# Gelus and casts moved behind the kept sums in three short pairs, and the down projection's sums taken half by half

## The chip, the cores and the metric

The kernel runs on one core of a Trainium2 chip. The metric is the device time of one execution in microseconds (us), as the median of several runs. Five engines work side by side, each through its own list of instructions: TensorE (PE in the profile; PEld is its loading of weights), VectorE (DVE), ScalarE (ACT), GpSimd (POOL) and SyncE (SP), which issues most of the DMAs. Matmuls write into PSUM, eight banks of 512 float32 columns for each of 128 partitions; VectorE and ScalarE read the banks.

## What is computed

One layer of a decoder on 1024 prompt positions and 64 sample positions (T = 1088 columns): attention in a sliding window, a gated branch beside it, and a feed-forward block with a convolution. Only the last one is touched here. From the reference, cut down:

```
def conv_ffn(h, w_up, conv_w, conv_b, w_down, prev):
    z = h @ w_up
    zp = jnp.concatenate([prev, z], axis=1)
    c = conv_b + sum(zp[:, j:j + T] * conv_w[j] for j in range(CONV_W))
    a, b = jnp.split(c, 2, axis=-1)
    return (jax.nn.gelu(a) * b) @ w_down, zp[:, T:]
```

with a model width of 1024, a hidden width of 2 x 2816 and a convolution of width 3. All data are float32.

## The kernel before

**Precision.** Each matmul operand is split into a high and a low part (`split`, line 39): ScalarE casts the high part (line 40), VectorE takes the difference (line 41). Each product is then three matmuls: high by high, high by low, low by high.

**The up projection.** The 2816 hidden rows of each half are 22 tiles of 128 rows; tile f of the first half and tile f of the second make a *pair*, `za` and `zb`. The two are worked out together by a scheme of seven products in place of eight (Winograd's form of Strassen's), in the class `Chain`. A chain works on one group of columns: group 0 has 576 columns (moving operands of 288), group 1 has 512 (moving operands of 256). Product j is 4 x 3 = 12 matmuls (line 301) into one of three PSUM banks, by the letters "adadaca": the first, third, fifth and seventh product add up in bank a, the second and fourth in bank d. Since the third adds to what the first left in a, the first's value has to be copied out before; this is a *kept sum*, copied by ScalarE in `keep` (lines 282 and 284). So the third product waits for the keep of the first, the fourth for that of the second, the fifth for that of the third, and the last for that of the fifth. The other products end in sums of VectorE or GpSimd (line 289) or scaled copies of ScalarE (line 319).

**Pairs with only the second group.** For the pairs f = 0, 1 and 2 (`FEW` is 3) the first group is worked out early, while the second group's input is still being made, and is stored to DRAM (`zd`). In the main loop (line 1756) the pairs go in the order 3 to 8, 0, 9 to 14, 1, 15 to 21, 2. A pair of the main loop runs two chains, 24 matmuls per product; pairs 0, 1 and 2 load their first half back (line 1764) and run the chain of group 1 alone, 12 matmuls per product.

**After each pair** `finish` (line 1729) runs the convolution on `za` and on `zb` (`conv`, line 1678: small copies of state by GpSimd, a scaled copy by ScalarE on line 1683, two steps of VectorE on lines 1684 and 1685), the Gelu of the first (lines 1734 and 1737, ScalarE), the product with the second (lines 1739 and 1740, VectorE), and stores the gated values to DRAM (`td`), at every second pair with the sums that the down projection's scheme of seven needs. `side_loads` issues copies of cache rows from DRAM to DRAM for f = 2 to 9. For the last two pairs `finish` is put off into the down projection.

**The down projection** is again seven passes in place of eight (order 5, 0, 2, 4, 6, 1, 3), each over 11 units. For a unit a tile of gated values is loaded (`t_upto`, line 1588: loads run ahead, then the split into `th` and `tl`) and multiplied with four blocks m of weights, each in two column halves e of 288 and 256 columns (`mm_dn`, line 1803). The first two and the last two units of a pass are taken together, in two rounds `mp` of two blocks each. At the end of a pass `take` (line 1808) adds the banks into the result `x` (VectorE, line 1814); the next pass writes the same banks. `dn_pools` (line 1582) opens the pools for this stage before the last pair of the up projection, loads the first four tiles and splits the first two.

**What sets the order.** The code is traced in order; a framework lays out each engine's list from it, with the code's order as priority and by its own reckoning of when things become ready, and it puts in every wait. `W.get` prepares the weights of coming products, with casts on ScalarE and sums on VectorE, so these stand between the instructions described here. `tc.issue_after(x)` binds what is traced under it to come behind x on x's engine.

Of the kernel before, what the change touches and what calls it, by code (L numbers as in the profile page):

```python
# [6 lines left out]
F32 = mybir.dt.float32  # L7
F32R = mybir.dt.float32r
I32 = mybir.dt.int32
AF = mybir.ActivationFunctionType  # L10
ALU = mybir.AluOpType
# [4 lines left out]
P = 128  # L16
D = 1024
KD = 8
NS = 64
NPR = 1024  # L20
T = NS + NPR
HT = T // 2
# [4 lines left out]
NFF = 22  # L27
# [7 lines left out]
def layer(tc, a):  # L35
    nc = tc.nc
    V, S, G, PE = nc.vector, nc.scalar, nc.gpsimd, nc.tensor

    def split(hi, lo, src):
        S.copy(hi, src)  # L40
        V.tensor_sub(lo, src, hi.bitcast(F32))  # L41
# [5 lines left out]
    with ExitStack() as top:  # L47
# [3 lines left out]
        td = [dram.tile([P, 7, HT], F32, name=f"td_{i}") for i in range(NFF // 2)]  # L51
# [3 lines left out]
        def gap(pool, nbytes):  # L55
            if nbytes:
                pool.tile([P, nbytes // 4], F32, name="gap", bufs=1)
# [195 lines left out]
        def right(stack, name, bufs=1):  # L253
            return stack.enter_context(tc.tile_pool(name=name, bufs=bufs, side="right", reuse_waits="tile"))
# [16 lines left out]
        class Chain:  # L271
# [7 lines left out]
            def keep(self, name, src, by=1.0):  # L279
                t = self.keeps.tile([P, 288], F32, name="k" + name.replace("n", "u"), bufs=3 if name in "un" else 2)[:, :self.n2]  # L280
                if by == 1.0:
                    S.copy(t, src)  # L282
                else:
                    S.activation(t, src, AF.Copy, scale=by)  # L284
                self.kept[name] = t
# [66 lines left out]
        apart = ("g", KD - 1, KD - 1)  # L352
# [6 lines left out]
        with ExitStack() as ph1:  # L359
# [61 lines left out]
            order = [*range(FEW, 9), 0, *range(9, 15), 1, *range(15, NFF), 2]  # L421
# [630 lines left out]
            for at, (pair, gs, whole) in enumerate(seq):  # L1052
                if at == 6:
# [3 lines left out]
                chains = [Chain(g, txa, psa, kpa, lambda e, half, g=g, n2=groups[g]["n"] // 2: (  # L1057
                    (zs[g][e][:, n2 * half:n2 * half + n2], 0, n2),)) for g in gs]
# [390 lines left out]
            held = {}  # L1449
# [11 lines left out]
            for c in range(KD):  # L1461
                for at, go in enumerate(merge(1, c, operand(1)) if c > 1 else [none, none, *first[c][2:]]):
                    if at == 1:
                        t, u = held.pop(c)
# [117 lines left out]
        def dn_pools():  # L1582
            dnp["t"] = right(tops, "tq")
            dnp["s3"] = own["s3"] = right(tops, "s3")
            t_upto(4, 2)
            gap(dnp["t"], 128)

        def t_upto(loads, splits):

            for n in range(len(ts["raw"]), min(loads, 7 * (NFF // 2))):  # L1590
                j, i = DN_ORDER[n // (NFF // 2)], n % (NFF // 2)
                raw = dnp["t"].tile([P, 576], F32, name="traw", bufs=4)[:, :HT]
                nc.sync.dma_start(raw, td[i][:, T_AT[j]])
                ts["raw"].append(raw)
            for n in range(len(ts["made"]), min(splits, 7 * (NFF // 2))):
                th, tl = (dnp["t"].tile([P, 576], F32R, name=x, bufs=5)[:, :HT] for x in ("th", "tl"))
                split(th, tl, ts["raw"][n])
                ts["made"].append((th, tl))
# [3 lines left out]
        def pool2(name, bufs, **kw):  # L1602
            return ph2.enter_context(tc.tile_pool(name=name, bufs=bufs, reuse_waits="tile", **kw))
# [56 lines left out]
        def side_loads(f):  # L1660
            with tc.issue_after(W.last.ins):
                if 2 <= f < 10:
                    nc.sync.dma_start(a["ks"][f - 2], a["ck"][f - 2, 8:128, :])
                    nc.sync.dma_start(a["vso"][f - 2], a["cvd"][f - 2, 8:128, :])
# [10 lines left out]
        def up_chain(g, za, zb):  # L1675
            return Chain(g, tx, psu, up, lambda e, half: z_parts((za, zb)[e], g, half))
# [14 lines left out]
        def z_pair():  # L1691
            return [zp["z"].tile([P, zp["n"]], F32, name=x, bufs=n) for x, n in (("za", zp.get("za", 1)), ("zb", 1))]

        def put_state(f, zs):
            for e, z in enumerate(zs):
                G.tensor_copy(z[:, 0:90].rearrange("p (b t) -> p b t", t=10)[:, :, 0:2],
                              stc[:, f + e * NFF])

        rest = []
        for f in range(FEW):  # L1700
            za, zb = z_pair()
# [18 lines left out]
        tmp = pool2("tmp", 1)  # L1720
# [5 lines left out]

        later, held = [], {}

        def finish(f, za, zb):
            at = order.index(f)  # L1730
            i = at // 2
            ca = conv(f, za)
            gt = za[:, 0:T]
            S.activation(gt[:, NS:T], ca[:, 80:1104], AF.Gelu_apprx_tanh)
            samp = lambda x: x[:, 0:80].rearrange("p (b t) -> p b t", t=10)[:, :, 0:8]
            gts = gt[:, 0:NS].rearrange("p (b t) -> p b t", t=8)
            S.activation(gts, samp(ca), AF.Gelu_apprx_tanh)
            cb = conv(f + NFF, zb)
            V.tensor_mul(gts, samp(cb), gts)
            V.tensor_mul(gt[:, NS:T], cb[:, 80:1104], gt[:, NS:T])  # L1740
            g2 = gt.rearrange("p (h t) -> p h t", h=2)
            if at % 2 == 0:
                nc.sync.dma_start(td[i][:, 0:2], g2)
                held["q"] = g2
            else:
                q, t2 = held["q"], tmp.tile([P, 2, HT], F32, name="t2")
                V.tensor_sub(t2[:, 0], g2[:, 0], g2[:, 1])
                V.tensor_sub(g2[:, 1], q[:, 1], g2[:, 1])
                V.scalar_tensor_tensor(t2[:, 1], g2[:, 1], -1.0, g2[:, 0], ALU.mult, ALU.subtract)
                V.scalar_tensor_tensor(q[:, 0], t2[:, 1], -1.0, q[:, 0], ALU.mult, ALU.subtract)  # L1750
                nc.sync.dma_start(td[i][:, 2:4], g2)
                nc.sync.dma_start(td[i][:, 4:6], t2)
                nc.sync.dma_start(td[i][:, 6], q[:, 0])
            side_loads(f)

        for at, f in enumerate(order):
            if at == NFF - 1:
                t0o.close()
                dn_pools()
                zp.update(z=right(tops, "z2"), za=1)  # L1760
            za, zb = z_pair()
            if f < FEW:
                for e, z in enumerate((za, zb)):
                    nc.sync.dma_start(z[:, 0:594], zd[f][e])
            else:
                put_state(f, (za, zb))
            chains = [up_chain(g, za, zb) for g in ((1,) if f < FEW else (0, 1))]
            for j in range(7):
                w = W.get(3, 1)
                for ch in chains[::1 - 2 * ((7 * at + j) % 2)]:  # L1770
                    ch.product(j, w)
                if f < FEW and j == 3:
                    put_state(f, (za, zb))
            if at < NFF - 2:
                finish(f, za, zb)
            else:
                later.append(lambda f=f, za=za, zb=zb: finish(f, za, zb))
        pse.close()

        with ExitStack() as ph3:  # L1780
# [3 lines left out]
            NU = NFF // 2  # L1784
# [136 lines left out]
            for at, j in enumerate(DN_ORDER):  # L1921
                new, last, n0 = j in (5, 0, 1), at == 6, at * NU
                blocks = [(0, 2), *((x, x + 1) for x in range(2, NU - 4 if last else NU - 2))]
                if not last:
                    blocks.append((NU - 2, NU))
                for lo, hi in blocks:
                    if at == 0:
                        if lo in (2, 5):
                            later.pop(0)()
                        if lo == 8:  # L1930
                            nc.sync.dma_start(a["tails"], stc)
                            ph2.close()
                            own["s2"], own["a22"] = pool3("s2", 1), pool3("a22", 1)
                            xp, lp = pool3("xp", 1), pool3("lp", 1)
                            acc += [lp.tile([P, HT], F32, name=f"acc{th}") for th in range(2)]
                            x_load(0, 0)
                    for go in hooks.get((at, lo), ()):
                        go()
                    got = units(n0 + lo, hi - lo)
                    for mp in range(2) if hi - lo == 2 else (0,):  # L1940
                        for e in range(2):
                            for x in range(lo, hi):
                                for m in range(2 * mp, 2 * mp + 2) if hi - lo == 2 else range(4):
                                    mm_dn(m, e, x, got[x - lo], new)
                        if hi == NU:
                            for m in (2 * mp, 2 * mp + 1):
                                for e in range(2):
                                    take(j, m, e)
            got = units(7 * NU - 4, 4)

# [45 lines left out]
NSTG, FEW, NPRE = 4, 3, 2  # L1996
# [86 lines left out]
```

## Time and profile before

| what | us |
|---|---|
| median of 3 runs | 1504.83 |
| the three runs | 1504.61, 1504.83, 1505.7 |
| the profiled execution, its own time | 1506.5 |
| its span from first to last instruction | 1504.6 |
| TensorE busy in it | 1492.3 |
| VectorE, ScalarE, GpSimd busy | 1163.4, 832.7, 282.5 |

A row of the timeline has the start, the duration, the engine, the line in the kernel, the operation, then output <- inputs with their shapes, and a count where equal instructions follow one another. In square brackets stands how long the engine was idle before, and what it waited for. Pair 0 of the main loop begins at 961 us, pair 1 at 1096, pair 2 at 1251; the down projection starts at 1261. A row of the table by stretches has, for each engine, the busy time and in brackets the number of instructions, then the granted clock, the DMA share and GB/s.

### The profile page before, as it was taken

The numbers are of one execution on the slowest core, as the hardware profiler recorded it, in microseconds if no ns is written. First come the engines' busy times: TensorE is split into PE (matmuls) and PEld (weight loads), VectorE is DVE, ScalarE is ACT, GpSimd is POOL, SyncE is SP. The second block draws the span as 40 slices with busy tenths as digits, with TensorE's granted clock in tenths as the row PEclk, the third lists the DMA queues.
The fourth block names the chain that finished last, engine by engine and source line by source line (L and its number), as shares of the span: only waits on it lengthen the run. The fifth ranks groups of instructions, "written<-read, shape, count | busy, mean of one in ns | idle before, by whom it ended". The sixth has DMA issues, their size and how long they took to land.

```text
span 1504.6 us, 31437 instructions
## 1 busy us (share of the span) xinstructions
PE 1492.3 (99%) x12169; PEld 1479.7 (98%) x12169; DVE 1163.4 (77%) x1954; ACT 832.7 (55%) x1798; POOL 282.5 (19%) x438
## 2 busy tenths in 40 slices
PE   9999999999999999999999999999999999999998
PEld 8999999999998999999999999999999999999998
DVE  6887779557545986988678888898898888785676
ACT  7656674554554775864444654654555556453463
POOL 2001003100030332430222222232142122000003
PEclk9999999999999999999999999999999999999999
DMA  8552468557659757859977423332332217973454
GB/s 282 182 189 104 165 216 270 176 177 249 216 209 326 236 177 237 246 190 315 337 242 271 142 102 121 119 123 95 116 131 95 109 64 243 362 235 98 121 185 134
DMA packets 136932, 286.10 MB, mean 190 GB/s; under 512 B 15312, under 2 KB 43856, under 8 KB 136784
## 3 DMA queue, kind: packets, MB, share of 16 engines
q1 hardware_dynamic: 131952, 279.57, 55.1%
q10 hardware_dynamic: 4832, 4.54, 0.9%
q8 instruction: 95, 1.56, 0.4%
q14 instruction: 53, 0.43, 0.1%
HBM read 195.56 MB, written 90.46 MB: 190 GB/s over the span
## 4 chain that ended last, share of the span: by engine, by line
PE 94%; DVE 3%; ACT 1%; issue 1%; DMA 0%; SPq 0%; DVEq 0%; ACTq 0%
PE st L301 52%; PE mm L241 15%; PE dn L1804 15%; PE st L538 6%; PE sc L1295 1%; PE po L1356 1%; PE mx L904 1%; PE pt L1328 1%; ACT s L1318 1%; DVE nm L1311 0%; DVE s L1321 0%; DVE s L1305 0%; DMA wh<-xt 0%; PE st L603 0%; DVE of L1367 0%
## 5 line engine op out<-in xcount | busy, mean ns | idle before, releaser
L301 PE MATMUL st<-th,wh 128*128 128x256 f32 (+1 forms) x2128 | 611.4, 287 | 0.3 <-ACT k L282 0.2
L301 PE MATMUL st<-tl,wh 128*128 128x256 f32 (+1 forms) x2128 | 609.7, 287 | 0.0
L301 PE MATMUL st<-th,wl 128*128 128x256 f32 (+1 forms) x2128 | 609.3, 286 | 0.0
L301 PEld LDWEIGHTS st<-th,wh 128*128 128x128 f32 x2128 | 400.6, 188 | 1.3 <-ACT k L282 0.9
L301 PEld LDWEIGHTS st<-th,wl 128*128 128x128 f32 x2128 | 400.9, 188 | 0.0
L301 PEld LDWEIGHTS st<-tl,wh 128*128 128x128 f32 x2128 | 400.4, 188 | 0.0
L40 ACT CAST wh<-wraw 128x512 fp32r<-128x512 f32 (+1 forms) x244 | 144.1, 611 | 85.3 <-PE st L301 33.6
L41 DVE TENSOR_TENSOR wl<-wraw,wh 128x512 fp32r<-128x512 f32 (+1 forms) x244 | 166.1, 696 | 27.3 <-ACT wh L40 25.4
L1804 PE MATMUL dn<-th,wh 128*128 128x288 f32 (+1 forms) x616 | 177.6, 288 | 0.0
L1804 PE MATMUL dn<-tl,wh 128*128 128x288 f32 (+1 forms) x616 | 177.1, 287 | 0.0
L1804 PE MATMUL dn<-th,wl 128*128 128x288 f32 (+1 forms) x616 | 177.0, 287 | 0.0
L40 ACT CAST wh<-ws 128x512 fp32r<-128x512 f32 x160 | 98.0, 622 | 96.5 <-PE st L301 78.3
L41 DVE TENSOR_TENSOR wl<-ws,wh 128x512 fp32r<-128x512 f32 x160 | 109.0, 694 | 50.4 <-ACT wh L40 48.7
L1804 PEld LDWEIGHTS dn<-th,wh 128*128 128x128 f32 x616 | 116.9, 190 | 0.0
L1804 PEld LDWEIGHTS dn<-th,wl 128*128 128x128 f32 x616 | 115.8, 188 | 0.0
L1804 PEld LDWEIGHTS dn<-tl,wh 128*128 128x128 f32 x616 | 115.8, 188 | 0.0
L289 POOL TENSOR_TENSOR z<-ku,k 128x256 f32<-128x256 f32 (+1 forms) x32 | 30.1, 943 | 317.2 <-ACT ku L284 242.4
L40 ACT CAST th<-traw 128x544 fp32r<-128x544 f32 (+1 forms) x85 | 54.1, 643 | 55.6 <-PE dn L1804 42.9
L41 DVE TENSOR_TENSOR tl<-traw,th 128x544 fp32r<-128x544 f32 (+1 forms) x85 | 61.0, 725 | 23.3 <-ACT th L40 23.1
L241 PE MATMUL mm<-s,wh 128*128 128x256 f32 (+1 forms) x384 | 76.5, 295 | 0.0
L282 ACT COPY k<-st 128x256 f32<-128x256 f32 (+1 forms) x152 | 56.0, 381 | 35.2 <-PE st L301 34.2
L241 PE MATMUL mm<-oh,wh 128*128 128x256 f32 (+1 forms) x256 | 73.6, 288 | 0.0
(311 smaller groups left out, 3187.2 us busy)
## 6 DMA issues: line engine op xcount, KB each, us to landing
wraw<-wt SPq DMA_DIRECT2D x133, 512.0 KB
traw<-td SPq DMA_DIRECT2D x77, 272.0 KB
td<-za SPq DMA_DIRECT2D x22, 544.0 KB
wraw<-wt SPq DMA_DIRECT2D x35, 256.0 KB
upd<-hl SPq DMA_DIRECT2D x14, 512.0 KB
td<-t SPq DMA_DIRECT2D x11, 544.0 KB
qd<-q SPq DMA_DIRECT2D x8, 576.0 KB
q<-qd SPq DMA_DIRECT2D x8, 576.0 KB
```

What stands on the lines that cost most here:

```text
L40: S.copy(hi, src)
L41: V.tensor_sub(lo, src, hi.bitcast(F32))
L241: PE.matmul(ps[:, lo:lo + c1 - c0], u[:, k, :], v[:, c0:c1], start=(clear and k == 0 and i == 0), stop=(k == nk - 1 and i == 2), skip_grou ...
L282: S.copy(t, src)
L289: op(to, pick(x, to, lo, hi), pick(y, to, lo, hi))
L301: PE.matmul(ps, u[:, kk, :], v, start=first and kk + i == 0, stop=kk == 3 and i == 2, skip_group_check=True)
L538: PE.matmul(ps, u, v[:, k, :], start=k + i == 0, stop=k == KD - 1 and i == 2)
L904: PE.matmul(ps[:, P * i:P * i + P], vn[:, i], late["wst"][:, c, :], start=True, stop=True)
L1295: PE.matmul(ps[:, h, o0:256], q, kst[kv][:, e, k0:cur + P], start=e == 0, stop=e == 1)
L1318: S.activation(s[:, h], s[:, h], AF.Exp, bias=nm[:, h:h + 1], accum_out=dn[:, h:h + 1])
L1328: PE.transpose(pt[:, h * P:h * P + P], s[:, h, 0:P], ident)
L1804: PE.matmul(place(m, e), u[:, m, :], v[:, lo:hi], start=new and i + k == 0 and (e == 0 or m != 1), stop=i == NU - 1 and k == 2, skip_group ...
```

## The change

Four things are edited:

- `finish` gets a way of being stopped half-way (`apart`). For the pair ahead of one that has only the second group, the convolutions are traced where they were, but the Gelus, the products, the stores and `side_loads` are returned as a function `close`. The loop calls it in the next pair, behind that pair's first product, bound to come behind the keep of the first product (`chains[0].last`). This is so for pairs 8 and 14, ahead of pairs 0 and 1. Pair 21, ahead of pair 2, is one whose `finish` is put off as before.
- `dn_pools` still loads the first four tiles of gated values, but no longer splits the first two of them; the splits are traced in pair 2 behind the keep of its first product, in the same way.
- With that the pool's small gap tile is taken ahead of the tiles of the split values.
- In the down projection the sums at the end of a pass are traced behind each column half: for a round of two blocks m, first both sums of half 0 behind the matmuls of half 0, then both of half 1. Before, all four came behind the matmuls of both halves, block by block.

```
             def keep(self, name, src, by=1.0):
...
-                    S.copy(t, src)
+                    self.last = S.copy(t, src)
...
         def dn_pools():
...
-            t_upto(4, 2)
+            t_upto(4, 0)
             gap(dnp["t"], 128)
...
-        def finish(f, za, zb):
+        def finish(f, za, zb, apart=False):
...
+            def gates():
+                S.activation(gt[:, NS:T], ca[:, 80:1104], AF.Gelu_apprx_tanh)
+                S.activation(gts, samp(ca), AF.Gelu_apprx_tanh)
+
+            if not apart:
+                gates()
             cb = conv(f + NFF, zb)
+
+            def close():
+                if apart:
+                    gates()
+                V.tensor_mul(gts, samp(cb), gts)
+                V.tensor_mul(gt[:, NS:T], cb[:, 80:1104], gt[:, NS:T])
...
+                side_loads(f)
+
+            if apart:
+                return close
+            close()
+
+        apart = []
         for at, f in enumerate(order):
...
                 for ch in chains[::1 - 2 * ((7 * at + j) % 2)]:
                     ch.product(j, w)
+                if f < FEW and j == 0:
+                    with tc.issue_after(chains[0].last.ins):
+                        if apart:
+                            apart.pop()()
+                        if at == NFF - 1:
+                            t_upto(4, 2)
...
             if at < NFF - 2:
-                finish(f, za, zb)
+                if order[at + 1] < FEW:
+                    apart.append(finish(f, za, zb, True))
+                else:
+                    finish(f, za, zb)
...
                                     mm_dn(m, e, x, got[x - lo], new)
-                        if hi == NU:
-                            for m in (2 * mp, 2 * mp + 1):
-                                for e in range(2):
+                            if hi == NU:
+                                for m in (2 * mp, 2 * mp + 1):
                                     take(j, m, e)
```

More of the change, by code (lines that the diff above doesn't have):

```diff
@@ L1733, in finish @@
             gt = za[:, 0:T]
-            S.activation(gt[:, NS:T], ca[:, 80:1104], AF.Gelu_apprx_tanh)
             samp = lambda x: x[:, 0:80].rearrange("p (b t) -> p b t", t=10)[:, :, 0:8]
             gts = gt[:, 0:NS].rearrange("p (b t) -> p b t", t=8)
-            S.activation(gts, samp(ca), AF.Gelu_apprx_tanh)
-            cb = conv(f + NFF, zb)
-            V.tensor_mul(gts, samp(cb), gts)
-            V.tensor_mul(gt[:, NS:T], cb[:, 80:1104], gt[:, NS:T])
-            g2 = gt.rearrange("p (h t) -> p h t", h=2)
@@ L1742, in finish @@
[L1742 to L1753, printed above, removed]
@@ L1754, in finish @@
-            side_loads(f)
+            def gates():
[3 more added lines that the diff above has]
+                gates()
+            cb = conv(f + NFF, zb)
+            def close():
[3 more added lines that the diff above has]
+                V.tensor_mul(gt[:, NS:T], cb[:, 80:1104], gt[:, NS:T])
+                g2 = gt.rearrange("p (h t) -> p h t", h=2)
+                if at % 2 == 0:
+                    nc.sync.dma_start(td[i][:, 0:2], g2)
+                    held["q"] = g2
+                else:
+                    q, t2 = held["q"], tmp.tile([P, 2, HT], F32, name="t2")
+                    V.tensor_sub(t2[:, 0], g2[:, 0], g2[:, 1])
+                    V.tensor_sub(g2[:, 1], q[:, 1], g2[:, 1])
+                    V.scalar_tensor_tensor(t2[:, 1], g2[:, 1], -1.0, g2[:, 0], ALU.mult, ALU.subtract)
+                    V.scalar_tensor_tensor(q[:, 0], t2[:, 1], -1.0, q[:, 0], ALU.mult, ALU.subtract)
+                    nc.sync.dma_start(td[i][:, 2:4], g2)
+                    nc.sync.dma_start(td[i][:, 4:6], t2)
+                    nc.sync.dma_start(td[i][:, 6], q[:, 0])
+                side_loads(f)
@@ L1774, in layer @@
             if at < NFF - 2:
-                finish(f, za, zb)
+                if order[at + 1] < FEW:
+                    apart.append(finish(f, za, zb, True))
+                else:
+                    finish(f, za, zb)
             else:
```

## The prediction

> **What bounds the kernel now.** I read the span and clock first, then the busy shares, then the chain that ended last.
>
> ```profile
> core 0: 1504.6 us, clock 0.998
> PE 1492.3 (99%) x12169; PEld 1479.7 (98%) x12169; DVE 1163.4 (77%) x1954; ACT 832.7 (55%) x1798; POOL 282.5 (19%) x438
> PE 94%; DVE 3%; ACT 1%; issue 1%; DMA 0%; SPq 0%; DVEq 0%; ACTq 0%
> ```
>
> TensorE is busy 99% of the span at full granted clock and holds 94% of the chain. So an edit that adds and removes no matmul can pay only in two ways: by closing holes in TensorE's stream, or by altering the spacing of its matmuls. The edit touches two places, the pairs that have only the second group (0, 1 and 2 in the list of pairs) and the sums of the down projection. I looked for holes there in the timeline of TensorE, by the distance from one matmul's start to the next, because a busy column hides holes shorter than a matmul's modelled tail.
>
> ```profile
> 965.48 0.28 PE L301 MATMUL st<-th,wl 128*128 128x256 f32 x1
> 965.75 0.39 PE L301 MATMUL st<-th,wh 128*128 128x256 f32 x1
> 965.98 0.28 PE L301 MATMUL st<-tl,wh 128*128 128x256 f32 x1
> ...
> 1099.69 0.28 PE L301 MATMUL st<-th,wh 128*128 128x256 f32 x1
> 1100.06 0.39 PE L301 MATMUL st<-th,wh 128*128 128x256 f32 x1
> 1100.28 0.28 PE L301 MATMUL st<-tl,wh 128*128 128x256 f32 x1
> ...
> 1104.61 0.29 PE L301 MATMUL st<-tl,wh 128*128 128x288 f32 x1
> 1104.90 0.39 PE L301 MATMUL st<-th,wh 128*128 128x256 f32 x1
> 1105.12 0.28 PE L301 MATMUL st<-tl,wh 128*128 128x256 f32 x1
> ...
> 1254.45 0.28 PE L301 MATMUL st<-th,wl 128*128 128x256 f32 x1
> 1254.96 0.38 PE L301 MATMUL st<-th,wh 128*128 128x256 f32 x1 [0.24 <-ACT k L282]
> 1255.19 0.28 PE L301 MATMUL st<-tl,wh 128*128 128x256 f32 x1
> ...
> 1259.72 0.28 PE L301 MATMUL st<-th,wl 128*128 128x256 f32 x1
> 1259.91 0.39 PE L301 MATMUL st<-th,wh 128*128 128x256 f32 x1
> 1260.13 0.28 PE L301 MATMUL st<-tl,wh 128*128 128x256 f32 x1
> ```
>
> The undisturbed distance comes from the down projection, where twelve 256-column matmuls lie between the first two starts below (1.41/12 = 0.118 us) and twelve between the last two (1.36/12 = 0.113 us).
>
> ```profile
> 1263.01 0.28 PE L1804 MATMUL dn<-th,wh 128*128 128x256 f32 x1
> 1264.42 0.30 PE L1804 MATMUL dn<-th,wh 128*128 128x288 f32 x1
> ...
> 1461.56 0.28 PE L1804 MATMUL dn<-th,wh 128*128 128x256 f32 x1
> 1462.92 0.30 PE L1804 MATMUL dn<-th,wh 128*128 128x288 f32 x1
> ```
>
> Each hole is the excess of two distances, since the matmul behind the late one is slow too. With 0.113 as the undisturbed one: 0.50 − 0.23 = 0.27 us in pair 0, 0.59 − 0.23 = 0.36 and 0.51 − 0.23 = 0.28 us in pair 1, 0.74 − 0.23 = 0.51 and 0.41 − 0.23 = 0.18 us in pair 2. The sum, **1.60 us**, is all that these places can give back as holes; it is 0.11% of the span. A measurement of this kernel can tell about 0.2%, 3.0 us, from no change.
>
> **Why the holes are there.** The third product of a pair adds into the bank of the first, and the fourth into that of the second, so each needs ScalarE's copy (a keep, line 282) of what stood there. A pair with both groups has 24 matmuls per product, a pair with the second group alone 12, some 1.4 us. ScalarE's timeline around the three pairs:
>
> ```profile
> 962.25 1.31 ACT L1683 ACTIVATE c<-zb,cw 128x1104 f32<-128x1104 f32 x1
> 963.46 0.35 ACT L282 COPY k<-st 128x256 f32<-128x256 f32 x1
> ...
> 964.23 1.06 ACT L1734 ACTIVATE za<-c 128x1024 f32<-128x1024 f32 x1
> ...
> 965.34 0.36 ACT L282 COPY k<-st 128x256 f32<-128x256 f32 x1
> ...
> 1097.35 1.32 ACT L1683 ACTIVATE c<-zb,cw 128x1104 f32<-128x1104 f32 x1
> 1098.56 1.05 ACT L1734 ACTIVATE za<-c 128x1024 f32<-128x1024 f32 x1
> ...
> 1099.65 0.63 ACT L282 COPY k<-st 128x256 f32<-128x256 f32 x2
> ...
> 1252.25 1.31 ACT L1683 ACTIVATE c<-zb,cw 128x1104 f32<-128x1104 f32 x1
> 1253.47 1.18 ACT L40 CAST th<-traw 128x544 fp32r<-128x544 f32 x2
> 1254.55 0.63 ACT L282 COPY k<-st 128x256 f32<-128x256 f32 x2
> ```
>
> In pair 0 the first keep already stands ahead of the Gelus; it is the second, at 965.34, that is late. In pair 1 both keeps stand behind both Gelus, in pair 2 behind two casts of gated values. So ScalarE's list does not follow the code strictly, and the first lesson is that one of the three cases is already as the change wants it.
>
> **Pair 0, Gelus behind the first keep.** The order that the change asks for (keep, then Gelus) is the one at 963.46 and 964.23. The second keep may stay behind the Gelus as now. I take 0. At best the Gelus come behind the second keep as well: 0.27 us gained. At worst one more cast comes between (two casts of pair 2 take 1.08 us from 1253.47 to 1254.55, one 0.54), and the hole grows by 0.5 us.
>
> **Pair 1, the same.** The keep takes the place of the Gelu: 1098.56, plus 0.35 for it, plus the 0.06 from the end of the keep (1099.65 + 0.35 = 1100.00) to the matmul at 1100.06, gives 1098.97. When would TensorE want it?
>
> ```profile
> 1098.67 0.28 PE L301 MATMUL st<-th,wh 128*128 128x256 f32 x1
> 1253.89 0.28 PE L301 MATMUL st<-th,wh 128*128 128x256 f32 x1
> ```
>
> These are the starts of the third dozen of matmuls in pairs 1 and 2. From 1098.67 to the hole at 1100.06 TensorE runs eleven more, 1.39 us of work that doesn't need the first keep: a later product of the pair has been put ahead of the third. That product is then missing as cover further on, and the keep of the fifth product becomes the hole at 1104.90. With the keep ready early I expect the products in code order. The third then waits 1098.97 − 1098.67 = 0.30, with its slow second matmul (0.22 − 0.11) 0.41 us, and the later hole closes: 0.36 + 0.28 − 0.41 = **0.23 us** gained. If the order of products stays, the first hole closes and the second doesn't: 0.36. All of it would be 0.64; the low end is 0.36 − 0.41 = −0.05, if the second hole stays all the same.
>
> The second keep then comes behind the Gelus. Two keeps take 0.63 and one 0.35, so the first holds ScalarE for 0.28; the Gelus hold it for 1.09 (1098.56 to 1099.65). The second keep thus starts at 1099.93 and lets the fourth product go at 1100.34. That is due 12 matmuls behind 1098.97, at 1100.33: level, and any delay there would be paid in full.
>
> **Pair 2, casts behind the first keep.** The keep moves to 1253.47 and lets the third product go at 1253.47 + 0.35 + 0.06 = 1253.88; it is due at 1253.89. The hole of 0.51 closes. Two casts follow, and the second keep lets the fourth product go at 1253.47 + 0.28 + 1.08 + 0.35 + 0.06 = 1255.24; it is due at 1253.89 + 1.36 = 1255.25, covered by a hair. With the third product in its place the hole of 0.18 goes as well: **0.69 us**; 0.2 at the least if a late second keep eats most of it, 0.69 at the most. The casts themselves come about 0.3 us later and are wanted first by the down projection, whose first matmul starts after 1261: 6 us of cover.
>
> **What else moves, at no cost.** VectorE's products with the Gelus, and the stores of the gated values, move behind the next pair's loads of kept halves on SyncE's queue:
>
> ```profile
> 1102.14 0.33 SPq L1764 DMA_DIRECT2D zb<-zd  x1
> 1103.89 0.33 SPq L1743 DMA_DIRECT2D td<-za  x1
> ```
>
> They stand in that order already, and the stored halves are read by the down projection, over 150 us later. The two copies of cache rows that follow pair 8 (line 1663) have no reader in the kernel. No state copy of GpSimd moves. The small gap tile is now taken ahead of the cast gated values, which then lie 128 bytes further; no row shows a cost or gain of that, and I take 0 with the pace rivals below as its bounds.
>
> **Sums half by half.** Per column block the four sums of two blocks are asked for after each half, so the second block's first-half sum no longer stands behind the first block's second half. VectorE's sums at the end of the first pass, and TensorE's start of the next:
>
> ```profile
> 1290.46 0.45 DVE L1814 TENSOR_TENSOR x<-x,dn 128x288 f32<-128x288 f32 x1
> 1292.03 1.11 DVE L1814 TENSOR_TENSOR x<-x,dn 128x288 f32<-128x288 f32 x3
> 1294.36 0.30 PE L1804 MATMUL dn<-th,wh 128*128 128x288 f32 x1
> ```
>
> One sum moves from 1292 or later to about 1291, while its bank is written again only after 1294.36. A release that is 1 us or more ahead becomes 2 us ahead. The whole stretch has no wait in it:
>
> ```profile
> 1262.00:1442.00 180.00, 180.00 (x1445) 180.00 (x1445) 130.85 (x226) 83.10 (x147) 0.00 (x0) 1.00 0.63 210
> ```
>
> TensorE is busy 180.00 of 180.00 us. The gain is 0; a loss would need a sum that is taken later than now, and none is.
>
> **The sum.** 0 + 0.23 + 0.69 + 0 = 0.92 us. The profiled execution took 1506.5 us (span 1504.6 and 1.9 around it), so it would take 1505.6; the median of the runs, 1504.83, is 1.7 lower, and I forecast **1503.9 us**, 0.06% faster, which counts as no change. Bounds of the terms: −0.5 − 0.05 + 0.2 = −0.35, and 1.60: 1505.2 to 1503.2.
>
> **Rivals.** *The pace of TensorE becomes the quicker one.* The same 256-column matmul of the down projection runs at 0.118 us apart at 1263 and at 0.113 apart at 1461, in the same loop. What decides between them no row shows; a hole taken from just ahead of the down projection could decide it anew. In the six passes before the last there are 6 × 11 × 4 × 3 = 792 such matmuls; 792 × (1.41 − 1.36)/12 = 3.3 us, so 1500.6. For it: the change removes the holes right ahead of 1261. Against it: the slow pace held for 190 us and nothing in the diff asks for it. Chance 0.22.
>
> The Trainium skill, "TensorE: Matmul & The Clock Gate", section "Back-to-back issue gap", gives one gap for one shape, N/2.4 + 2.5 ns, an estimate of 109 ns at 256 columns. By it there is no second pace, this rival falls away and 1503.9 stands alone; the two distances above disagree with it, and the measurement decides.
>
> *The slower pace takes over the pairs (ends slower).* From pair 0 to the last there are 16 pairs with 7 × 12 = 84 such matmuls each. If a moved hole set all of them from 0.113 to 0.118, that would cost 16 × 84 × 0.05/12 = 5.6 us: 1509.5. It decides from about seven tenths of them on, where 3.9 us outweigh the 0.9 gained by 3.0. Against it: the holes of pairs 0 and 1 stand in this stage now, and the change adds none of another kind. Chance 0.05.
>
> *The change does not do what it says in ScalarE's list.* If the keeps stay behind the Gelus, or the second keep becomes the hole wherever the first is mended, nothing is gained: 1504.8. For it: pair 0, where the keep is ahead of the Gelus and the hole is there all the same, and the two covers of under 0.1 us above. Chance 0.23.
>
> **How the numbers follow.** My forecast keeps 0.50. Forecast and last rival are both within 0.2%: 0.73 with rounding; faster 0.22; slower 0.05. The range must reach the quicker pace to hold 8 in 10: 1500.4 (3.3 and 0.2 off 1503.9) to 1505.2. The likeliest case's own range is 1503.2 to 1505.2.
>
> **What would show it.** In ScalarE's timeline a keep right behind the convolution's first step of zb in pairs 1 and 2; in TensorE's, no distance over 0.3 us near 1254 and near 1104, one of about 0.3 us or none near 1099, and that of pair 0 unchanged. In the down projection still no wait and 180 us for the same matmuls. I am wrong if the hole in pair 0 closes, if new holes of 0.3 us or more appear in pairs 1 and 2 at the fourth product, or if the down projection's 256-column matmuls are 0.113 apart from the start.

## The result, and the profile after

The changed kernel takes **1508.27 us** in the median of 8 runs (1507.12 to 1510.67), the kernel before 1504.61 beside it (8 runs, 1503.43 to 1506.23): ratio 1.0025, 95% interval 1.0015 to 1.0035. It is slower by 3.7 us, outside the range of the prediction. Span and clock, busy shares and the chain of the profile after:

```profile
core 0: 1505.8 us, clock 0.998
PE 1493.4 (99%) x12169; PEld 1481.0 (98%) x12169; DVE 1163.4 (77%) x1954; ACT 832.3 (55%) x1798; POOL 280.2 (19%) x438
PE 94%; DVE 4%; ACT 1%; issue 1%; DMA 0%; DVEq 0%; ACTq 0%
```

As many instructions on every engine, TensorE as busy as before; nothing here says where 3.7 us went. First the holes. TensorE's timeline around the three pairs:

```profile
965.61 0.28 PE L301 MATMUL st<-th,wl 128*128 128x256 f32 x1
965.88 0.39 PE L301 MATMUL st<-th,wh 128*128 128x256 f32 x1
966.10 0.28 PE L301 MATMUL st<-tl,wh 128*128 128x256 f32 x1
...
1098.35 0.28 PE L301 MATMUL st<-th,wl 128*128 128x256 f32 x1
1098.76 0.39 PE L301 MATMUL st<-th,wh 128*128 128x256 f32 x1
1098.99 0.28 PE L301 MATMUL st<-tl,wh 128*128 128x256 f32 x1
...
1253.67 0.37 PE L301 MATMUL st<-th,wh 128*128 128x256 f32 x1
1253.88 0.28 PE L301 MATMUL st<-tl,wh 128*128 128x256 f32 x1
...
1259.11 0.28 PE L301 MATMUL st<-th,wl 128*128 128x256 f32 x1
1259.70 0.39 PE L301 MATMUL st<-th,wh 128*128 128x256 f32 x1 [0.32 <-ACT ku L284]
1259.93 0.28 PE L301 MATMUL st<-tl,wh 128*128 128x256 f32 x1
```

Taken as in the prediction, pair 0 has 0.49 − 0.23 = 0.26 us (0.27 before), pair 1 has 0.64 − 0.23 = 0.41 in one hole (0.36 and 0.28 before), pair 2 has 0.21 − 0.11 = 0.10 and 0.82 − 0.23 = 0.59 (0.51 and 0.18). In sum 1.36 us for 1.60: the moved keeps give back 0.24. ScalarE's timeline of pairs 1 and 2 tells why:

```profile
1097.14 1.31 ACT L1683 ACTIVATE c<-zb,cw 128x1104 f32<-128x1104 f32 x1
1098.35 0.36 ACT L282 COPY k<-st 128x256 f32<-128x256 f32 x1
1098.60 1.07 ACT L1738 ACTIVATE za<-c 128x1024 f32<-128x1024 f32 x1
...
1253.26 0.35 ACT L282 COPY k<-st 128x256 f32<-128x256 f32 x1
1253.51 1.19 ACT L40 CAST th<-traw 128x544 fp32r<-128x544 f32 x2
...
1258.32 1.06 ACT L1738 ACTIVATE za<-c 128x1024 f32<-128x1024 f32 x1
1259.28 0.37 ACT L284 ACTIVATE ku<-st 128x256 f32<-128x256 f32 x1
```

The first keeps stand ahead of the Gelu and of the casts, as asked for. But in pair 2 a Gelu of a put-off `finish` runs at 1258.32, ahead of the keep of the fifth product, for which the last product waits until 1259.70. Before, they stood in that order too, in ScalarE's timeline at

```profile
1257.48 1.07 ACT L1734 ACTIVATE za<-c 128x1024 f32<-128x1024 f32 x1
...
1259.47 0.38 ACT L284 ACTIVATE ku<-st 128x256 f32<-128x256 f32 x1
```

but there half of the sixth product had been put ahead of the third, so the fifth ended late: the last six matmuls ahead of 1259.91 are the other half of the sixth, which puts its end near 1259.15 (1259.72 less five distances of 0.113), when this Gelu was done. Now the products run in code order, the fifth is done when the sixth starts,

```profile
1257.86 0.28 PE L301 MATMUL st<-th,wh 128*128 128x256 f32 x1
```

and its keep stands behind casts of weights and the Gelu for 1.4 us (1257.86 to 1259.28).

The time is lost further on, in the down projection, where no hole is to be seen. The same stretch as the prediction showed (there x1445), for the kernel after:

```profile
1262.00:1442.00 180.00, 180.00 (x1439) 180.00 (x1438) 129.86 (x224) 82.03 (x146) 0.00 (x0) 1.00 0.63 210
```

Six matmuls fewer, 6 × 0.125 = 0.8 us, without a wait and at a granted clock of 1.00. And the profile before was itself of one of the longer executions of its kernel, as a second profile of the same program showed (below). From the start of its first matmul to that of its last the stage takes 233.8 us before (1261.43 to 1495.20) and 235.3 after (1261.22 to 1496.47): 1.5 us more, where the two spans differ by 1.2. So matmuls that lie further apart are all of the difference between these two profiles, and the question is what moved them apart.

### The profile page after: what moved, and what is told of

The parts are those of the page before. It is cut to its first block, busy times and chain, and to the rows that moved or that the text cites. A ratio compares the mean times of both kernels' runs of the same rounds, so it can differ in the third digit from the quotient of the medians.

```text
span 1505.8 us, 31430 instructions
## 1 busy us (share of the span) xinstructions
PE 1493.4 (99%) x12169; PEld 1481.0 (98%) x12169; DVE 1163.4 (77%) x1954; ACT 832.3 (55%) x1798; POOL 280.2 (19%) x438
## 4 chain that ended last, share of the span: by engine, by line
PE 94%; DVE 4%; ACT 1%; issue 1%; DMA 0%; DVEq 0%; ACTq 0%
PE st L301 51%; PE dn L1827 15%; PE mm L241 15%; PE st L538 6%; PE sc L1295 1%; PE po L1356 1%; PE mx L904 1%; PE pt L1328 1%; ACT s L1318 1%; DVE nm L1311 0%; DVE s L1305 0%; DVE s L1321 0%; PE st L603 0%; DVE of L1367 0%; DVE pl L41 0%
```

## The experiments

Two theories. **Place**: the change takes the gap tile ahead of the split gated values `th` and `tl`, which puts them 128 bytes further (`th` at 206272 in place of 206144 in each partition), and there TensorE reads more slowly. **Pace by entry**: the spacing is set by how the stream enters the down projection, so by the moved keeps. A third one, the sums, was settled by the instruction lists alone: with only that edit every engine's list is the same as before, waits included. The sums had been put in the order of their readiness before.

**addr**, the place alone:

```
-            t_upto(4, 2)
+            t_upto(4, 0)
             gap(dnp["t"], 128)
+            t_upto(4, 2)
```

> The kernel before with its gap tile taken between the loads and the splits of dn_pools: every engine's list has the order of the kernel before, only the split gated values th and tl lie 128 bytes further on, as in the changed kernel. Theory of place (the 128 bytes make TensorE's reads or the neighbours' writes slower in the down projection): 1508.3 us, +3.7 on the kernel before, and matmuls of the down projection over 1% further apart than before. Theory of pace by entry (the spacing in the down projection is set by how the stream enters it, so by the moved keeps): 1504.6, no change, for the entry is unmoved.

Measured: 1510.23 us against 1506.25, ratio 1.0026 (1.0015 to 1.0037). The place alone makes a loss as large as the whole one.

**gap_back**, the changed kernel with the old place:

```
-            gap(dnp["t"], 128)
...
                             t_upto(4, 2)
+                            gap(dnp["t"], 128)
```

> The changed kernel with its gap tile taken behind the splits, so that th and tl lie where they lay before; the order of every engine's list is that of the changed kernel. Theory of place: the moved keeps alone remain, about 1504.0 (0.3 to 0.9 us under the kernel before). Theory of pace by entry: as the changed kernel, 1508.3.

Measured: 1505.70 against 1506.25, ratio 0.9999 (0.9990 to 1.0009). The moved keeps alone neither gain nor lose what can be told. Pace by entry falls as the cause.

**halves** and **no_halves**, each the same program under another name: halves adds this edit to the kernel before, no_halves takes it back from the changed one.

```
                             for x in range(lo, hi):
...
-                        if hi == NU:
-                            for m in (2 * mp, 2 * mp + 1):
-                                for e in range(2):
+                            if hi == NU:
+                                for m in (2 * mp, 2 * mp + 1):
                                     take(j, m, e)
```

> The kernel before with only the sums of the down projection taken half by half. Every engine's list of instructions comes out the same, word for word, as without it: the sums stood in the order of their readiness already. All theories: 1504.6, and the scatter of its runs against the kernel before is the scatter of one program against itself. Its profile is a second look at the program of before: if its down projection has another spacing than the first look's, the spacing varies from run to run.

> The changed kernel with the sums taken as before. Again the lists are those of the changed kernel, word for word, so all theories say 1508.3 (+3.7). Its profile is a second look at the changed program: theory of place expects the same wide spacing again (288 columns at 0.133, 256 at 0.118); pace by entry allows another one.

Measured: halves 1506.06, ratio 1.0002 (0.9992 to 1.0012); no_halves 1509.99, ratio 1.0026 (1.0017 to 1.0034). The sums do nothing, and the scatter between two names of one program is a tenth of the loss. Their profiles are second executions of the kernels before and after. The table by stretches from 1270 to 1440 us, first for the kernel before, then halves, then the kernel after, no_halves, addr and gap_back; what counts is the number of TensorE's matmuls in 170 us:

```profile
1270.00:1440.00 170.00, 170.00 (x1365) 170.00 (x1365) 120.98 (x213) 76.18 (x137) 0.00 (x0) 1.00 0.62 207
```

```profile
1270.00:1440.00 170.00, 170.00 (x1387) 170.00 (x1386) 124.40 (x217) 78.20 (x140) 0.00 (x0) 1.00 0.63 209
```

```profile
1270.00:1440.00 170.00, 170.00 (x1359) 170.00 (x1358) 120.83 (x212) 77.27 (x137) 0.00 (x0) 1.00 0.63 208
```

```profile
1270.00:1440.00 170.00, 170.00 (x1360) 170.00 (x1359) 122.52 (x214) 76.62 (x137) 0.00 (x0) 1.00 0.62 207
```

```profile
1270.00:1440.00 170.00, 170.00 (x1360) 170.00 (x1359) 120.98 (x212) 77.10 (x138) 0.00 (x0) 1.00 0.62 206
```

```profile
1270.00:1440.00 170.00, 170.00 (x1387) 170.00 (x1386) 124.89 (x217) 78.08 (x140) 0.00 (x0) 1.00 0.64 212
```

All are busy 170 of 170 us, yet the old place gets 1387 matmuls through (halves, gap_back) and the new one 1359 or 1360. 170/1387 = 0.1226 us and 170/1360 = 0.1250 us apart, times the 1848 matmuls of the stage: 4.4 us. The stage as a whole says the same: 230.9 us in halves (1262.10 to 1493.02), 235.3 in the kernel after. The first profile of the kernel before caught an execution with 1365, 0.1245 apart, so beside it the profile after seems only 0.8 us worse. Two of the 256-column halves, in halves and in the kernel after:

```profile
1263.68 0.28 PE L1804 MATMUL dn<-th,wh 128*128 128x256 f32 x1
1265.04 0.29 PE L1804 MATMUL dn<-th,wh 128*128 128x288 f32 x1
```

```profile
1262.82 0.28 PE L1827 MATMUL dn<-th,wh 128*128 128x256 f32 x1
1264.23 0.29 PE L1827 MATMUL dn<-th,wh 128*128 128x288 f32 x1
```

Twelve matmuls in 1.36 us, 0.113 apart, at the old place; 1.41, 0.118, at the new.

**m256, m128, s64, tl128**: which places are slow? All have the lists of the kernel before. m256 has a gap of 384 bytes behind the split tiles, m128 one of 256, s64 has 64 ahead and 64 behind, and tl128 has the 128 between `th` and `tl`. First m256, then tl128:

```
-            gap(dnp["t"], 128)
+            gap(dnp["t"], 384)
```

```
             t_upto(4, 2)
-            gap(dnp["t"], 128)
...
-                th, tl = (dnp["t"].tile([P, 576], F32R, name=x, bufs=5)[:, :HT] for x in ("th", "tl"))
+                th = dnp["t"].tile([P, 576], F32R, name="th", bufs=5)[:, :HT]
+                if n == 0:
+                    gap(dnp["t"], 128)
+                tl = dnp["t"].tile([P, 576], F32R, name="tl", bufs=5)[:, :HT]
```

> The kernel before with its gap tile 384 bytes long in place of 128, so that th, tl, the raw tiles and the sums of weights below them lie 256 bytes lower; same order of every list. Theory of residue (what counts is where in a block of 256 bytes th and tl start: 64 before, 192 after): no change, ratio 1.000, 256-column matmuls of the down projection 0.113 apart. Theory that any move off the old place costs (a fixed neighbour or an absolute place): ratio about 1.0025, 0.118 apart.

> The same with a gap of 256 bytes: everything named lies 128 bytes lower, so th and tl start at 192 in a block of 256 again, but in the other direction from the place before. Theory of residue: ratio 1.0026, 256 columns 0.118 apart and 288 at 0.133. Theory that only the move upward (nearer to the edge) costs: 1.000.

> 64 of the 128 bytes of gap ahead of th and tl, 64 behind: they start at 128 in a block of 256, and the 256-column half of a tile (1152 bytes on) at 0. Nothing else moves. Theory of residue with the 256-column half as the one that counts (quick at 192, slow at 64): a new value; if starts at a block's edge are the best, 0.113 or under and ratio 0.998 to 1.000; if the cost grows with the distance from the old place, half of it, 1.0013.

> The gap between th and tl: the low parts tl alone lie 128 bytes further, the high parts th where they were. One of three matmuls reads tl. If the reads of each matmul's own operand cost, a third of it: 256 columns at 0.1148 in the mean with every third at 0.118, ratio 1.0009. If all of a stream takes one pace by where it stands as a whole: 1.000 or 1.0026.

Measured, beside 1505.80 for the kernel before: m256 1505.82, ratio 1.0000 (0.9990 to 1.0010); m128 1509.16, 1.0029 (1.0018 to 1.0040); s64 1510.85, 1.0038 (1.0025 to 1.0052); tl128 1511.29, 1.0038 (1.0025 to 1.0052). The table by stretches, in the same order:

```profile
1270.00:1440.00 170.00, 170.00 (x1387) 170.00 (x1386) 122.96 (x215) 78.06 (x139) 0.00 (x0) 1.00 0.63 207
```

```profile
1270.00:1440.00 170.00, 170.00 (x1360) 170.00 (x1359) 121.50 (x213) 77.35 (x138) 0.00 (x0) 1.00 0.62 205
```

```profile
1270.00:1440.00 170.00, 170.00 (x1353) 170.00 (x1353) 121.45 (x211) 77.03 (x137) 0.00 (x0) 1.00 0.62 204
```

```profile
1270.00:1440.00 170.00, 170.00 (x1350) 170.00 (x1349) 121.21 (x211) 76.75 (x137) 0.00 (x0) 1.00 0.62 203
```

256 bytes lower is the old pace to the matmul (1387), 128 lower the pace of the changed kernel (1360). So it is neither a fixed neighbour nor the distance, but where the tiles start within 256 bytes. My guesses for the other two were wrong: half the shift costs no less than the whole one (1353 matmuls for 1360; the intervals of the times overlap), and so does moving the low parts alone (1350), where I had expected a third.

**swap, swap128**: which operand counts? The two column halves are cut the other way, so that the 256 columns start where the tile starts:

```
-            spans = ((0, 288), (288, HT))
+            spans = ((256, HT), (0, 256))
...
-                V.tensor_add(acc[1][:, 288:HT], acc[1][:, 288:HT], x)
+                V.tensor_add(acc[1][:, 0:256], acc[1][:, 0:256], x)
```

swap128 has the edit of addr as well.

> The kernel before with the two column halves of the down projection cut the other way: the 288 columns are 256 to 543, the 256 columns 0 to 255 of each tile. No address moves; the 256-column operand now starts where its tile starts, at 64 in a block of 256 bytes, the 288-column one 1024 bytes on, at 64 too, as before. Theory that the start of the 256-column operand counts (quick at 192, slow at 64): 256 columns 0.118 apart, 288 unchanged at 0.132, ratio 1.002 to 1.0025. Theory that the place of the tile counts, whatever is read of it: 0.113 and ratio 1.000.

> The same cut with the tiles 128 bytes further, where the changed kernel has them. Theory of the 256-column operand's start: it is at 192 again, so 0.113 apart, and the changed place costs nothing any more, ratio 1.000 (288 columns at 0.1325 to 0.133 may leave 0.0003). Theory of the tile's place: 0.118, ratio 1.0026.

Measured, beside 1505.36: swap 1508.60, ratio 1.0021 (1.0011 to 1.0031); swap128 1508.92, 1.0022 (1.0012 to 1.0031). The table by stretches for the two:

```profile
1270.00:1440.00 170.00, 170.00 (x1363) 170.00 (x1362) 121.72 (x213) 77.12 (x138) 0.00 (x0) 1.00 0.62 205
```

```profile
1270.00:1440.00 170.00, 170.00 (x1368) 170.00 (x1367) 122.34 (x214) 77.73 (x138) 0.00 (x0) 1.00 0.62 205
```

Swap came out as the theory of the operand's start has it: no tile moved and yet it is slow. That points to the columns that TensorE reads, and not to the neighbours of the tiles or the writing of them; the sums and results are cut the other way along with it, and that was not tried alone. Swap128 came out as neither theory has it: its time fits that of the tile's place, which swap has just contradicted, and its pace fits neither. Its timeline over two units:

```profile
1333.03 0.28 PE L1805 MATMUL dn<-th,wh 128*128 128x256 f32 x1
1334.39 0.29 PE L1805 MATMUL dn<-th,wh 128*128 128x288 f32 x1
1335.99 0.28 PE L1805 MATMUL dn<-th,wh 128*128 128x256 f32 x1
1337.40 0.30 PE L1805 MATMUL dn<-th,wh 128*128 128x288 f32 x1
```

The 256 columns take 1.36 us in one unit (1333.03 to 1334.39) and 1.41 in the next (1335.99 to 1337.40). The two take turns in this way, unit by unit, through the first six passes, though all these operands start at 192. With the start at 192 the quick pace is possible but not sure; what makes it turn is not shown.

**t1_128**: does the rule hold in another stage? The input of the second group in the up projection goes from 192 to 64 in a block of 256.

```
-        gap(t1p, 448)
+        gap(t1p, 320)
...
+                if kk == 3:
+                    t1p.tile([P, 32], F32, name="gap2", bufs=1)
```

> The kernel before with 128 bytes of gap moved from ahead of to behind the second group's split input of the up projection, which then starts at 64 instead of 192 in a block of 256; every list in the old order, every other tile where it was. Theory of the operand's start: the 256-column matmuls of the up projection go from 0.1144 to 0.1178 in the mean, 22 x 84 x 0.0034 = 6.3 us, ratio 1.0042; the down projection unchanged. Theory that something in the down projection alone makes the place matter: ratio 1.000.

Measured: 1509.78 beside 1505.36, ratio 1.0031 (1.0016 to 1.0046). A stretch of the up projection, in halves and in t1_128:

```profile
980.00:1080.00 100.00, 100.00 (x813) 100.00 (x812) 87.16 (x124) 54.98 (x110) 26.51 (x39) 1.00 0.31 109
```

```profile
980.00:1080.00 100.00, 100.00 (x806) 100.00 (x804) 86.21 (x124) 53.38 (x107) 26.73 (x39) 1.00 0.28 99
```

806 for 813 in 100 us: the loss is there too. The ratio is about three quarters of the one expected, but from four runs, and the profiled execution, 1514.24 us, was the longest of them; in it the down projection ran slowly as well (below), so how much of the time is the up projection's is open.

**best**, gap_back with the Gelus behind the second keep and the put-off ones behind the fifth product's:

```
-                    S.activation(t, src, AF.Copy, scale=by)
+                    self.last = S.activation(t, src, AF.Copy, scale=by)
...
-                if f < FEW and j == 0:
+                if f < FEW and j == 1:
...
-                            later.pop(0)()
+                            with tc.issue_after(chains[0].last.ins):
+                                later.pop(0)()
```

> The changed kernel with th and tl in their old place, the Gelus of pairs 8 and 14 behind the second keep of the next pair instead of the first, and the two put-off finishes bound behind the keep of the last pair's fifth product. If the holes are ScalarE's order and nothing else: the hole of pair 0 (0.27 us) and that of pair 2 near 1260 (0.5 us) close, pair 1 keeps about 0.3; ratio to the kernel before 0.9993, which the times can hardly tell from 1. If other work on ScalarE takes their place: new holes of 0.3 us or more in the same three pairs, ratio 1.000.

Measured: 1505.12 beside 1505.36, ratio 0.9995 (0.9986 to 1.0003). The holes of pair 0 and near 1260 are gone in its trace, pair 1 keeps its 0.41 us, and a new one stands at the end of the down projection's first pass, where TensorE waits for a sum of VectorE:

```profile
1293.77 0.28 PE L1827 MATMUL dn<-th,wl 128*128 128x256 f32 x1
1294.23 0.37 PE L1827 MATMUL dn<-th,wh 128*128 128x288 f32 x1 [0.19 <-DVE x L1837]
```

It is faster than the changed kernel was (1.0025 to the kernel before); against the kernel before it is no change that can be told.

## Why the prediction was wrong

**The step that failed** is the one on the gap tile: "no row shows a cost or gain of that, and I take 0 with the pace rivals below as its bounds." It measured about +3.9 us (0.0026 of 1506, addr), as much as the whole loss. The step saw the 128 bytes, and pace as a thing of its own, and did not join them. The rival that ends slower named the right means, a wider spacing without waits, but set it in the pairs, made holes its cause and gave it 0.05. The place of the tiles does it, in the down projection.

**What hid it** was the one profile of before. It ran at 0.1245 there, nearly the slow pace, so the down projection seemed to have nothing to lose and only 3.3 us to win. The hint stood in the times: that execution took 1506.5, 1.7 above the median. I took the difference off as if profiling cost it. The rival of the quicker pace, with its 0.22, rested on that one execution too: in halves, the same program, the quicker pace holds from the start of the stage. The profiled executions of halves, gap_back and m256 took 1504.28, 1504.14 and 1504.70, with 1387 matmuls in the stretch, 1.1 to 1.8 under the medians of their own runs.

**The holes**, term by term. Pair 0: 0 forecast, 0.27 and 0.26 measured, right. Pair 1: 0.23 forecast, 0.64 to 0.41, right to the hundredth, with the products back in code order and the second hole gone. Pair 2: 0.69 forecast, 0.69 to 0.69, wrong: the first hole shrank to 0.10, near the 0 worked out, but with the fifth product early again its keep found the put-off Gelu ahead of it. I had followed the first two keeps and taken the later hole for gone with the order of products; the cover of the fifth product's keep I had not worked out. The sum is 0.24 in place of 0.92; gap_back's 0.9999 agrees with either.

**The sums half by half**: 0 forecast, 0 measured, for a better reason than mine: the edit changes no instruction. The rival "the change does not do what it says" was true of this part, and I had not seen that it could be.

**Two rules against the runs.** Addr and halves have the same lists, and the same shape runs at other distances in them (0.118 and 0.113 us at 256 columns); so one gap per shape does not hold here. The prediction went too far in drawing that rule from the Trainium skill: "TensorE: Matmul & The Clock Gate", section "Back-to-back issue gap", gives the formula for an isolated matmul, and says that in a stream of weight loads and matmuls, as here, both set the spacing. The Trainium skill, "SBUF — State Buffer", section "Door 1: The DMA port swizzle (why `[64,N]` ≈ `[32,N]`)", says that SBUF has lines of 16 bytes and that a crossing into a new line costs. By that alone a shift by 128 or 64 bytes, a whole number of lines, would change nothing; addr (1.0026) and s64 (1.0038) disagree.

**What stays open**: how the start of an operand comes to set the pace. In halves, gap_back, m256 and best the old place ran at the quick pace. In the first profile of the kernel before it did not, nor in the down projection of t1_128, where the tiles lie at the old place:

```profile
1270.00:1440.00 170.00, 170.00 (x1365) 170.00 (x1364) 122.54 (x212) 78.92 (x140) 0.00 (x0) 1.00 0.63 210
```

In both of these the slow pace held for the first six passes and the quick one came with the last; in addr, after, no_halves and m128 the slow pace held to the end. So in the traces of this stage the quick pace is seen only with the 256 columns starting at 192, and swap128 shows that this start alone does not make it sure. No run shows what tips one execution.

## What to carry to other kernels

When TensorE is busy all the time, compare the number of its matmuls in a fixed stretch: here the spacing grew without any wait, and no busy share showed it. An edit that moves a tile is an edit of its own, even by 128 bytes and even if it only changes when a pool first meets a name; keep addresses fixed when an order is tried, or vary them alone. And where the profiled execution lies off the median, take a second profile before reading a pace from it.

## What the runs showed of the hardware

- The spacing of these matmuls (each with a weight load of its own) hung on where the moving operand starts in 256 bytes. In the down projection, with the 288-column and the 256-column operand at 64 and 192: 1387 matmuls in 170 us in three of six profiled executions and 1383 in best, which has a wait there, 1365 in two; at 192 and 64: 1360 (addr, m128, no_halves; 1359 after); at 64 and 64: 1363 (swap); at 192 and 192: 1368 (swap128); at 128 and 0: 1353 (s64); high and low parts at different places: 1350 (tl128).
- A shift by 256 bytes left the pace as it was (1387 in m256).
- The clock granted was 1.00 in all of these stretches, and TensorE was shown busy throughout, but for 0.19 us in best.
